# A convolution in Winograd form: the weights from two DMA queues, and two image loads made one

## The chip, the cores and the metric

The kernel runs on one core of one Trainium2 chip. The metric is the device time of one execution, in microseconds (us); the time of a kernel is the median of its runs. The kernel before takes 126.02 us, the median of three runs (125.92 to 126.29).

## The reference

`x` is 16 images of 64 channels of 64 x 64, `weight` is 128 x 64 x 3 x 3, both float32. The output is the ordinary 3 x 3 convolution with one pixel of zero padding, float32, 16 x 128 x 64 x 64:

```python
x_pad = np.pad(x, ((0, 0), (0, 0), (1, 1), (1, 1)), mode='constant')
for b in range(batch):
    for co in range(c_out):
        for ci in range(c_in):
            for kh in range(3):
                for kw in range(3):
                    output[b, co] += weight[co, ci, kh, kw] * x_pad[b, ci, kh:kh+h, kw:kw+w]
```

The input is 16.8 MB, the weights are 0.29 MB and the output is 33.6 MB.

## The kernel before

**Tiling.** Images are taken in eight pairs, p = 0 to 7. A pair fills the 128 partitions: 64 channels of one image and 64 of the next. Along the rows the kernel uses a Winograd form, which makes two output rows from sums, differences and outer differences of input rows, so that fewer matrix products are needed. Each pair is worked in two halves (h = 0 and 1), so there are 16 halves, in the order of the list `halves` (line 196).

**Memory.** One tile, `homes`, has eleven places of 16 KB for each partition. `X_HOME` says which place receives the input of a pair, and `O_HOME` which two places hold its two output images until they are stored. Places are used again: the output of a pair goes where the inputs of pairs already used were. The fifth pair (p = 4) and the sixth (p = 5) are loaded to the places 7 and 8, which lie next to each other.

**Loads.** At the start SyncE issues all the loads one behind the other on its DMA queue: the weights (line 66; output channel on the partition, 2304 bytes each), pair 0 in two parts (rows 0 to 33, and the rest), and pairs 1 to 7 whole, 2 MB each (line 71). That is ten transfers.

**Weights.** As soon as they are in, GpSimd (line 84) and ScalarE (line 85) each cast them to float16, TensorE transposes them (line 101), and ScalarE and VectorE build seven combinations of them in `Wt` (lines 147 to 158). In between VectorE makes the sums of the first half (line 112, from line 152), which the first matrix products need.

**A half.** GpSimd makes sums (line 112), differences (line 119) and outer differences (line 130) of a half, two halves ahead of its use. ScalarE casts some rows (line 140). TensorE does the products (line 178). ScalarE copies partial results from PSUM to the output's place (lines 245, 247, 249, 263), and VectorE combines (lines 260 to 262).

**Stores.** They are written out by hand in `stores` (line 213): nothing goes out before the half (2, 0). Then SyncE issues a store of half an image and one of a whole image; after (2, 1) four more; and from then on a pair at a time (`store_both`, line 207). The last seven rows of one image of pair 5 are stored by two transfers from ScalarE's queue (lines 252 and 253). The ones before are all on SyncE's queue, behind the loads.

**Order.** `keep` fixes the order of the instructions of each engine as written. The framework gives each transfer from SyncE or ScalarE one of eight semaphores in turn, in the order in which they stand in the program; a transfer that takes a semaphore again waits until the one that had it before has landed. So the ninth and tenth transfers wait for the first and the second.

Of the kernel before, what the change touches and what calls it, by code (L numbers as in the profile page):

```python
# [15 lines left out]
def kernel(  # L16
# [12 lines left out]
    nc = tc.nc  # L29
# [3 lines left out]
    NP = B // 2  # L33
    RB = 8

    keep = tc.keep_in_program_order
    x_rows = x.rearrange("b c h w -> (b c) h w")
    w_flat = weight.rearrange("co ci kh kw -> co (ci kh kw)")
# [13 lines left out]
    homes = slots.tile([128, 11, H, W], F32)  # L52
# [9 lines left out]
    def spared(at, n):  # L62
        return spare[:, at : at + n]

    w_raw = spared(0, CI * 9)
    keep(nc.sync.dma_start(w_raw, w_flat))

    def load(p, cuts=((0, H),)):
        for lo, hi in cuts:
            keep(  # L70
                nc.sync.dma_start(
                    xs[p][:, lo:hi, :], x_rows[128 * p : 128 * p + 128, lo:hi, :]
                )
            )

    load(0, ((0, 34), (34, H)))
    for p in range(1, NP):
        load(p)

    ident = spared(1920, 64).bitcast(F16)  # L80
# [214 lines left out]
```

## Time and profile before

| | |
|---|---|
| median of three runs | 126.02 us (125.92 to 126.29) |
| the profiled execution | 126.17 us |
| its span, first to last instruction or transfer | 124.3 us |
| busy: TensorE / VectorE / ScalarE / GpSimd | 95.5 / 63.6 / 81.3 / 90.6 us |
| moved by the DMA engines | 50.77 MB, mean 408 GB/s over the span |
| weights: issue, landing | 0.74 us, 3.5 us later |
| first matrix product of the convolution | 8.55 us |
| first store issued | 40.23 us |
| last matrix products end, last store issued | about 104.5 us, 105.82 us |

Times in the trace count from the start of the span. A busy time is that of one engine; the DMA share is the mean over the core's 16 DMA engines. A wait of an engine is put down to what ended last before it went on.

### The profile page before, as it was taken

How to read it: one execution, taken by the hardware profiler on the slowest of the kernel's cores; microseconds unless marked ns; L12 is line 12 of the kernel's file. 1: busy time of each engine (PE TensorE's matmuls, PEld its weight loads, DVE VectorE, ACT ScalarE, POOL GpSimd, SP SyncE). 2: the span in 40 equal slices, each digit the busy share in tenths (PEclk: the TensorE clock that was granted, in tenths of full speed). 3: DMA queues.
4: the chain of work that ended last, by engine and by line, in shares of the span. 5: the costliest groups of instructions: out<-in, count | busy, mean ns of one | idle time of the engine just before them, and what ended most of it. 6: DMA issues, size and time to landing. Idle time of an engine off the chain costs nothing.

```text
span 124.3 us, 2114 instructions
## 1 busy us (share of the span) xinstructions
PE 95.5 (77%) x873; PEld 49.8 (40%) x873; DVE 63.6 (51%) x56; ACT 81.3 (65%) x86; POOL 90.6 (73%) x52
## 2 busy tenths in 40 slices
PE   0329999999999998969999999999999996000000
PEld 0214555555455553534555555555555552000000
DVE  0099848393928472908294837556483939000000
ACT  4466798879697938659979797888888793000000
POOL 2209999999999999999999999999999700000000
PEclk9999999999999999999999999999999999655555
DMA  4999999999999999999999999999999999999980
GB/s 112 388 443 432 443 427 438 417 422 422 427 427 438 411 464 401 432 438 417 422 424 435 438 427 424 422 438 422 431 418 441 416 436 421 421 422 448 427 369 37
DMA packets 3954, 50.77 MB, mean 408 GB/s; under 512 B 360, under 2 KB 488, under 8 KB 744
## 3 DMA queue, kind: packets, MB, share of 16 engines
q1 hardware_dynamic: 3808, 50.40, 95.9%
q10 hardware_dynamic: 136, 0.23, 0.5%
q8 instruction: 7, 0.11, 0.3%
q14 instruction: 3, 0.02, 0.0%
HBM read 17.07 MB, written 33.55 MB: 407 GB/s over the span
## 4 chain that ended last, share of the span: by engine, by line
PE 68%; DMA 10%; DVE 4%; ACT 2%; POOL 1%; issue 0%; ACTq 0%; SPq 0%; DVEq 0%
PE acc L178 68%; DMA out_dram<-homes 7%; DMA homes<-in_weight_dram 3%; DVE homes L262 2%; DVE ss L112 1%; ACT homes L245 1%; ACT homes L247 1%; POOL homes L84 1%; DVE homes L149 0%; DVE Wt L150 0%; PE wp L101 0%; ACT homes L147 0%; ACTq L245 0%; SPq L200 0%; DVEq L150 0%
## 5 line engine op out<-in xcount | busy, mean ns | idle before, releaser
L178 PEld LDWEIGHTS <-Wt 64*128 64x128 f16 x864 | 48.8, 95 | 49.2 <-issue 5.3
L178 PE MATMUL acc<-xh,Wt 64*128 64x504 f16 (+3 forms) x384 | 45.9, 370 | 0.2
L112 POOL TENSOR_TENSOR ss<-homes 128x1024 f16<-128x1024 f32 x15 | 35.4, 2360 | 4.3 <-DMA homes<-in_x_dram 4.3
L260 DVE TENSOR_TENSOR homes<-acc,homes 128x1024 f32<-128x1024 f32 x16 | 19.6, 1224 | 34.9 <-PE acc L178 16.9
L130 POOL TENSOR_TENSOR ee<-homes 128x960 f16<-128x960 f32 (+1 forms) x15 | 35.3, 2350 | 0.0
L178 PE MATMUL acc<-ee,Wt 64*128 64x504 f16 (+1 forms) x192 | 26.5, 377 | 1.5 <-ACT homes L245 1.5
L178 PE MATMUL acc<-ss,Wt 64*128 64x504 f16 (+1 forms) x192 | 24.9, 392 | 2.3 <-DVE ss L112 2.3
L245 ACT COPY homes<-acc 128x1024 f32<-128x1024 f32 x16 | 16.2, 1012 | 10.1 <-DMA out_dram<-homes 4.6
L263 ACT COPY homes<-acc 128x1024 f32<-128x1024 f32 x16 | 16.3, 1017 | 8.5 <-PE acc L178 8.5
L262 DVE TENSOR_TENSOR homes<-homes,acc 128x1024 f32<-128x1024 f32 x16 | 19.5, 1219 | 1.0 <-PE acc L178 0.2
L119 POOL TENSOR_TENSOR dd<-homes 128x512 f16<-128x512 f32 x15 | 20.0, 1332 | 0.0
L261 DVE TENSOR_TENSOR homes<-acc,homes 128x1024 f32<-128x1024 f32 x16 | 19.4, 1214 | 0.0
L140 ACT CAST xh<-homes 128x1088 f16<-128x1088 f32 x16 | 17.9, 1118 | 0.1
L249 ACT COPY homes<-acc 128x1024 f32<-128x1024 f32 x16 | 16.5, 1030 | 0.0
L247 ACT COPY homes<-acc 128x1024 f32<-128x1024 f32 x16 | 16.3, 1017 | 0.3 <-PE acc L178 0.3
L178 PE MATMUL acc<-dd,Wt 64*128 64x504 f16 (+1 forms) x96 | 13.3, 379 | 0.0
L101 PE MATMUL wp<-homes 128*128 128x128 f16 x9 | 1.1, 312 | 5.1 <-POOL homes L84 5.1
L149 DVE SCALAR_TENSOR_TENSOR homes<-wp,homes 128x384 f32<-128x384 f32 x1 | 0.6, 558 | 6.1 <-ACT homes L147 6.1
L101 PEld LDWEIGHTS <-homes 128*128 128x128 f16 x9 | 0.9, 160 | 5.0 <-POOL homes L84 5.0
L84 POOL CAST homes<-homes 128x576 f16<-128x576 f32 x1 | 0.7, 662 | 3.0 <-DMA homes<-in_weight_dram 3.0
L130 DVE TENSOR_TENSOR ee<-homes 128x1088 f16<-128x1088 f32 x1 | 2.5, 2504 | 0.0
L85 ACT CAST homes<-homes 128x576 f16<-128x576 f32 x1 | 0.7, 671 | 2.3 <-DMA homes<-in_weight_dram 2.3
(17 smaller groups left out, 8.2 us busy)
## 6 DMA issues: line engine op xcount, KB each, us to landing
out_dram<-homes SPq DMA_DIRECT2D x5, 4096.0 KB, 21.2
homes<-in_x_dram SPq DMA_DIRECT2D x7, 2048.0 KB, 30.4
out_dram<-homes SPq DMA_DIRECT2D x4, 2048.0 KB, 16.6
out_dram<-homes SPq DMA_DIRECT2D x2, 1024.0 KB, 6.7
out_dram<-homes SPq DMA_DIRECT2D x1, 1824.0 KB, 20.8
homes<-in_x_dram SPq DMA_DIRECT2D x1, 1088.0 KB, 5.6
homes<-in_x_dram SPq DMA_DIRECT2D x1, 960.0 KB, 7.5
homes<-in_weight_dram SPq DMA_DIRECT2D x1, 288.0 KB, 3.5
```

The costliest lines, as they stand in the source:

```text
L112: keep(eng.tensor_add(t, v[:, j : j + 16, 0, :], v[:, j : j + 16, 1, :]))
L119: keep(eng.tensor_sub(t, v[:, j : j + RB, 1, :], v[:, j : j + RB, 0, :]))
L130: eng.tensor_sub(ees[p][:, lo - 16 : hi - 16, :], xs[p][:, lo - 1 : hi - 1, :], xs[p][:, lo + 1 : hi + 1, :],)
L140: keep(nc.scalar.copy(t, xs[p][:, C_ROW[h] : C_ROW[h] + 17, :]))
L178: nc.tensor.matmul(tiles[:, b2, lo:hi, c_lo:c_hi], Wt[p0 : p0 + 64, wi, kw, :], src[p0 : p0 + 64, first : last + 1 : step, c_lo + kw - 1 : ...
L245: keep(nc.scalar.copy(f1, pf1))
L247: keep(nc.scalar.copy(g1, pg1))
L249: keep(nc.scalar.copy(f0, pf2))
L260: keep(nc.vector.tensor_add(g1, pg2, g1))
L261: keep(nc.vector.tensor_add(f0, pf1, f0))
L262: keep(nc.vector.tensor_sub(f1, f1, pf2))
L263: keep(nc.scalar.copy(g0, pg1))
```

## The change

The weights are no longer one transfer of 128 output channels on SyncE's queue. SyncE loads the channels 0 to 63, and ScalarE's queue the channels 64 to 127. Pairs 4 and 5 are no longer two transfers of 2 MB: one transfer of 4 MB fills the places 7 and 8. The count of transfers up to the first store is ten in both kernels.

```diff
     w_raw = spared(0, CI * 9)
-    keep(nc.sync.dma_start(w_raw, w_flat))
+    for eng, lo in ((nc.sync, 0), (nc.scalar, 64)):
+        keep(eng.dma_start(w_raw[lo : lo + 64, :], w_flat[lo : lo + 64, :]))
...
     load(0, ((0, 34), (34, H)))
-    for p in range(1, NP):
+    for p in (1, 2, 3):
+        load(p)
+
+    two = x[8:12, :, :, :].rearrange("(q b) c h w -> (b c) q h w", b=2)
+    keep(nc.sync.dma_start(homes[:, 7:9, :, :], two))
+    for p in (6, 7):
         load(p)
```

## The prediction

> **What bounds the kernel now.** I read the page's rows of slices first, then the chain that ended last, and then asked for busy times by stage. The rows of slices, 40 equal parts of the span:
>
> ```profile
> PE   0329999999999998969999999999999996000000
> POOL 2209999999999999999999999999999700000000
> DMA  4999999999999999999999999999999999999980
> GB/s 112 388 443 432 443 427 438 417 422 422 427 427 438 411 464 401 432 438 417 422 424 435 438 427 424 422 438 422 431 418 441 416 436 421 421 422 448 427 369 37
> ```
>
> TensorE and GpSimd look full, but they are done by slice 34 (about 104 us), and the DMA engines are full from the second slice to the last but one. The span ends when the bytes have been moved. The queue table says whose bytes:
>
> ```profile
> q1 hardware_dynamic: 3808, 50.40, 95.9%
> q10 hardware_dynamic: 136, 0.23, 0.5%
> ```
>
> q1 is SyncE's queue: 50.40 MB of the 50.77, and 95.9% of sixteen engines' span. The chain of waits seems to contradict this, since its heads are TensorE 68% and DMA 10%:
>
> ```profile
> 31 pieces in order of time: start us, us, what
> ...
> 8.55 36.03 PE acc L178 x324
> 44.59 0.02 issue
> 44.61 1.23 DVE homes L262
> 45.84 0.02 SPq L200
> 45.86 0.04 issue
> 45.90 8.33 DMA out_dram<-homes
> ...
> 104.53 1.22 DVE homes L262
> ```
>
> The chain follows instructions back; it stops at the last vector instruction and says nothing of the 18 us of stores behind it. So I don't take TensorE as the bound, and ask the stages for the DMA share (last two columns):
>
> ```profile
> 1.00:2.00 1.00, 0.00 (x0) 0.00 (x0) 0.00 (x0) 1.00 (x1) 0.29 (x1) 1.00 0.29 25
> 2.00:3.00 1.00, 0.00 (x0) 0.00 (x0) 0.00 (x0) 0.01 (x1) 0.00 (x0) 1.00 0.94 266
> 20.00:30.00 10.00, 10.00 (x98) 5.11 (x94) 6.22 (x6) 8.12 (x10) 10.00 (x5) 1.00 1.00 426
> 40.00:42.00 2.00, 2.00 (x22) 1.03 (x20) 0.07 (x1) 2.00 (x3) 2.00 (x1) 1.00 0.96 410
> 120.00:121.00 1.00, 0.00 (x0) 0.00 (x0) 0.00 (x0) 0.00 (x0) 0.00 (x0) 0.50 0.61 262
> 122.00:123.00 1.00, 0.00 (x0) 0.00 (x0) 0.00 (x0) 0.00 (x0) 0.00 (x0) 0.50 0.04 16
> ```
>
> The engines are busy from 2 us on, also where the queue passes from loads to stores (40 to 42 us: 0.96), and they run dry one by one from 120 to 123 us. The trace also holds each DMA packet, which no view lists. From these records: the first weight packet starts at 1.76 us, 1.02 us after its issue at 0.74; a 16 KB packet takes 611 ns and the next one starts at its end; the engines finish between 120.1 and 123.0 us, the slowest alone after 122.6. Only three things can move the end: bytes, time in which an engine has no packet, and where the slowest engine's hiccups lie.
>
> **The frame of the sum.** The profiled execution took 126.17 us: span 124.3, and 1.87 around it. In the span: 1.76 until the first packet, 121.26 of packets on the slowest engine, 1.3 of completion and closing. The median of the runs, 126.02, is 0.15 lower; I add changes to the profiled time and take 0.15 off.
>
> **Bytes.** The same 0.29 MB of weights in packets of 2304 bytes, and the same 4 MB for pairs 4 and 5 in packets of 16 KB. One completion write more for the weights and one fewer for the pairs, 9 ns each per engine. Change: 0.
>
> **Merging pairs 4 and 5.** SyncE saves one issue (328 to 642 ns for the nine loads). All its issues are over at 7.2 us, with data queued until 44 us, so this is worth 0; were the queue empty, it would be worth those 0.3 to 0.6 us. The two pairs now land together:
>
> ```profile
> DMA to landing us min/median/max: 5.6/26.1/37.6
> ```
>
> That is line 71: the first part of pair 0 is issued at 1.18 and lands at 6.8, the last pair is issued at 6.83 and lands at 44.4. By the same view pair 4 lands at about 29.8 (issued 3.76, 26.1 later) and pair 5 at 34.7 (4.36 and 30.4). Pair 4 becomes visible 4.9 us later. Its first user is GpSimd's sum of half (4, 0), the eighth of line 112 on GpSimd, at 51.47 us: 16.8 us of cover. Without that cover the price would be 4.9 us. Is one transfer of 4 MB slower or faster than two of 2 MB? Nearest row: stores of 4 MB with the same pattern of two pieces per partition land every 9.7 us in the packet records, and stores of 2 MB every 4.86, so 0.0 per 4 MB, with ±0.1 for reading.
>
> The semaphores: pairs 6 and 7 are still the ninth and tenth transfers. Before, pair 7's issue waited 1.4 us for the first part of pair 0; now the two wait for the halves of the weights, at the latest 5.1 us (below). Behind them on SyncE's queue stand only the stores, from 40 us on, which keep landed semaphores. 0.
>
> The Trainium skill (DMA: Bandwidth & Descriptors, Anatomy of one DMA) fits a transfer as 2.0 us fixed plus bytes by rate, measured on the software path, and so would credit the merge with 2.0 us if transfers ran one after the other. By it the sum would be 124.0. The shares of 1.00 from 20 to 30 us, with several transfer boundaries in them, say that the fixed part lies under the neighbours' data here.
>
> **Splitting the weights.** SyncE's own issue: 0.39 us for 128 rows; for 64 rows I take 0.33 (the cheapest load) to 0.42. Pair 0's issue stays at 1.1 to 1.2 us. ScalarE now issues a transfer before its table load, which starts at 0.73, lasts 1.28 and is followed by 2.25 us of waiting for the weights. Its two late issues took 0.55 (124 channels) and 1.01 us (4 channels); the table load then ends at 2.6 to 3.0 us, before the cast at 4.26. Hidden; if the weights landed at 2.6 it would cost up to 0.4 on the path of the first product, nothing at the end.
>
> When do the weights land? Now at 4.24 us: fourteen of the sixteen engines have finished their eight rows by 3.25 us, the other two at 3.65 and 3.88, the rest is receipt. Best case, both halves start together at 1.76 and the stragglers vanish: 3.6. Worst case, ScalarE's issue takes 1.01 and its four rows per engine then alternate with packets of pair 0 (328 ns each, 93 for a row): 0.74+1.01+0.63+4x0.42 = 4.06, plus 0.36 of receipt and again one stall of the seen 0.7: 5.1. I take 4.2, no change.
>
> And what is it worth? The first product needs the weights' chain and VectorE's sum, which needs pair 0 (landed 6.8, sum started 7.28). Earlier weights therefore bring the first product forward by at most 0.47 us, later ones push it back one for one, at most 0.9 us. TensorE then runs without a gap to the first store (issued 40.23). With 1.02 from issue to packet that store could start at 41.25; the first engine comes free at 42.15 by the packet records, the slowest at 44.0. Spare: 0.90 us. A delay of 0.9 uses just that, and an earlier store waits for the loads. The next store that waits for products is issued at 45.90 and has its turn at 49.5: 2.6 us spare. All later ones have more (last store issued 105.82, its turn at 110.3). So the landing of the weights is worth 0 at the end in its whole range.
>
> The rule in the Trainium skill that speaks against this half (same page, Rules for kernel authors) is that two transfers to separate halves of the partitions share the same 16 engines and should be one transfer. The trace agrees as far as the shares of the second 2 to 3 us go (0.94 with one queue: there is no idle engine to use); by the rule the landing stays and the sum stays 0.
>
> **What is left is the ramp.** The eight rows of an engine need 8x0.093 = 0.74 us by their usual packet, but 1.2 to 1.5 us pass from the first packet to 2.94 to 3.25, because first packets take 0.14 to 0.70. This 0.45 to 0.75 us is the only piece of the stream that the change touches, and whatever happens to it moves everything behind it, all 121 us, by the same amount. Two queues could overlap their first packets (down to -0.45), or each have a ramp of its own (up to +0.6). Nothing in the trace shows two queues starting on an empty engine; where ScalarE's queue starts beside SyncE's (87.7 us), its packets take their usual 74 ns from the first on, without a pause. That row is the nearest, so I take 0, and keep both ends.
>
> Sum: 126.17 + 0 + 0 + 0 - 0.15 = 126.0.
>
> **Rivals.**
> A. No change, 126.0 (125.65 to 126.4): chance 0.62. 0.3% (0.38 us) is about what a measurement of this kernel can tell from no change; the three runs spread over 0.37.
> B. Slower: the ramp is paid twice. ScalarE's half starts behind, each engine pauses for a second first packet of up to 0.6 us, and the whole stream moves: 126.6 (126.4 to 127.0). It decides once the pause exceeds 0.38. For it: first packets of up to 0.70, and ScalarE's issues of up to 1.01. Against: pair 0 is already queued on SyncE's side from about 2.2 us, so an engine waiting for the other half has something to do. Chance 0.20.
> C. Faster: the ramps overlap and the two straggling engines (0.4 to 0.6 late) are gone: 125.5 (125.2 to 125.64). For it: the slowest engine sets the end, and its lag may come from there. Against: the stragglers at the start need not be the last ones at the end. Chance 0.16.
> D. Faster: the merge removes an exposed pause between two transfers. A transfer has 1.02 us from issue to its first packet and some 0.36 from its last packet to landing; if pair 5 had waited for both, the merge would save 1.4: 124.6. Against: the share of 1.00, which leaves no pause. Chance 0.02.
>
> **How the numbers follow.** The likeliest is A. To hold 8 in 10 the range takes most of B and C: 125.4 to 126.8. Faster 0.18 (C and D), same 0.62, slower 0.20.
>
> **What would show it.** In the profile after: q10 with 0.147 MB more and q1 with as much less; a 4 MB load; the DMA row again full from slice 2 on; weights landed at 3.6 to 5.1; first product at 8.1 to 9.4; first store issued at 39.8 to 41.1; the DMA share from 40 to 42 us still near 1; last store's data ending near 123. Wrong would be: the share from 2 to 3 us far below 0.94 (B) or clearly above (C), a hole at 42 us (then the spare of 0.90 was mis-sized), or a 4 MB load that takes other than 9.7 us.

## The result, and the profile after

The changed kernel takes 127.03 us (median of 14 runs), the kernel before 126.22 (14 runs beside it): 1.0047 times as long, interval 1.0029 to 1.0066. In a second set it was 1.0067 (1.0043 to 1.0091). The forecast was no change, 126.0, with a range up to 126.8. The changed kernel is slower by some 0.6 to 0.85 us.

Four of the 22 executions of the changed kernel took 128.9 to 129.9 us; the ratios, here and below, leave out such executions, and as the recorded profile is of one of them, the lines below are from the run e1, the same kernel profiled again (126.94 us, span 125.2), unless the text says otherwise. The line numbers after the loads are 6 higher than before (L118 for L112, L184 for L178).

First the rows of slices, then the two queues:

```profile
PE   0229999999999999969999999999999996000000
DMA  4999999999999999999999999999999999999991
...
q1 hardware_dynamic: 3728, 50.25, 95.5%
q10 hardware_dynamic: 216, 0.38, 0.9%
```

0.15 MB have moved from q1 to q10, as the diff says. The DMA engines are full as before; so the same bytes take longer. The timeline of the first 10 us shows what came first:

```profile
0.73 0.54 SPq L67 DMA_DIRECT2D homes<-in_weight_dram  x1
0.73 0.57 ACTq L67 DMA_DIRECT2D homes<-in_weight_dram  x1
...
3.43 1.28 ACT L91 ACT_TABLE_LOAD   x1 [3.43 <-DMA homes<-in_weight_dram]
...
4.72 0.67 ACT L91 CAST homes<-homes 128x576 f16<-128x576 f32 x1
...
5.54 1.15 PE L107 MATMUL wp<-homes 128*128 128x128 f16 x9 [5.54 <-ACT homes L91]
```

Each half of 64 channels is issued in 0.54 to 0.57 us, where all 128 took 0.39. And ScalarE's table load, which stood at 0.73 us before, now waits for weights: its idle time ends at 3.43 with the landing of the first half. The cast depends on two transfers now, and a wait for one of them has come to stand ahead of the table load. GpSimd's cast, which has no table load, starts at 3.93 us, when both halves are there; ScalarE's has to wait for the end of the load, 0.79 us longer: its cast starts at 4.72 (4.26 before), and the first product of the convolution at 9.01 (8.55 before). The chain that ended last has it word for word:

```profile
0.73 2.63 DMA homes<-in_weight_dram
...
3.43 1.28 ACT L91
4.71 0.01 issue
4.72 0.68 ACT homes L91
...
9.01 37.10 PE acc L184 x324
```

TensorE's 324 products up to the half (2, 1) take 37.10 us; before, 36.03. The first products, by the timeline of TensorE, after and then before:

```profile
9.01 2.75 PE L184 MATMUL acc<-ss,Wt 64*128 64x512 f16 x12 [2.32 <-DVE ss L118]
11.52 1.51 PE L184 MATMUL acc<-dd,Wt 64*128 64x512 f16 x6
12.80 2.00 PE L184 MATMUL acc<-xh,Wt 64*128 64x512 f16 x12
```

```profile
11.06 0.92 PE L178 MATMUL acc<-dd,Wt 64*128 64x512 f16 x6
11.81 1.47 PE L178 MATMUL acc<-xh,Wt 64*128 64x512 f16 x12
```

The products begin at about half their later speed in both kernels (a pair starts every 0.43 us, later every 0.22), and the slow stretch lasts longer after: the first pair at the later speed starts at 13.98 us, against 11.38. The granted clock is 1.00 in both, so the profile's clock row doesn't show it. The Trainium skill (TensorE: Matmul & The Clock Gate, Part 1) has a free-running window of activity behind such a start, so that the length of the slow stretch depends on where the first products fall in it; these runs agree in that the stretch differs from run to run, from 2.8 us (before) to 5.9 (e14, the kernel before with another order of stores), and do not show the window itself. The first store is issued at 41.75 us, 1.52 later than before: 0.46 from the first product and 1.06 from TensorE.

How much of this is the change's? Seven of the recorded kernels start like the kernel before: itself, e4, e5, e6, e9, e10 and e14. In the other six the casts of the weights start at 3.57 to 3.84 us and not at 4.26, the first product at 7.91 to 8.24 and not at 8.55, and the slow stretch lasts 3.3 to 5.9 us and not 2.8. e9 is one of them:

```profile
3.60 0.67 ACT L85 CAST homes<-homes 128x576 f16<-128x576 f32 x1 [1.59 <-DMA homes<-in_weight_dram]
...
7.98 2.74 PE L178 MATMUL acc<-ss,Wt 64*128 64x512 f16 x12 [2.41 <-DVE ss L112]
...
11.77 2.39 PE L178 MATMUL acc<-xh,Wt 64*128 64x512 f16 x12
```

So the profile before has the latest weights and the shortest slow stretch of the seven. Against their mean (8.13 us) the first product of the kernels with the halves on two queues and the late table load, e1, e11 and e13, comes 0.9 us later (8.97 to 9.08), and not 0.46. The slow stretch isn't longer in these three (4.2 us on the mean, against 4.3 in the seven), so the 1.06 us are scatter and not the change. VectorE has half (2, 0) ready for the first store at 39.84 to 41.08 us in the seven, and at 40.77 to 41.60 in the three.

At that point the spare of 0.90 us is gone. By the packet records the first engine has ended its loads at 42.44 (42.15 before), and the store's first packet starts at 42.59. So some engines wait, 0.03 us on the mean of the sixteen; in the DMA shares of a microsecond it can't be seen:

```profile
42.00:43.00 1.00, 1.00 (x14) 0.50 (x11) 0.00 (x0) 1.00 (x3) 1.00 (x2) 1.00 0.96 401
```

But from there on packets are longer: those of 16 KB last 621.2 ns on average up to 119 us (614.9 before), 107 for each engine, 0.67 us. The lengthening is spread from 44 to 112 us; from 112 to 119 us they last 613 ns in both kernels.

The sum, by the last packet of the slowest engine (124.00 against 123.02, 0.98 later): loads end 0.27 later on the mean of the engines because the first packet came at 2.05 and not at 1.76; the wait at the passage is 0.03 on the mean; the longer packets make 0.67. Together 1.0. The mean of the engines' ends is 1.16 later, so the account is good to some 0.2 us.

### The profile page after: what moved, and what is told of

It reads as the page before. It is cut to its first block, busy times and chain, and to the rows that moved or that the text cites. A ratio compares the mean times of both kernels' runs of the same rounds, so it can differ in the third digit from the quotient of the medians.

```text
span 128.1 us, 2117 instructions
## 1 busy us (share of the span) xinstructions
PE 98.0 (76%) x873; PEld 50.6 (40%) x873; DVE 64.8 (51%) x56; ACT 81.5 (64%) x86; POOL 90.8 (71%) x52
## 4 chain that ended last, share of the span: by engine, by line
PE 68%; DVE 6%; POOL 5%; ACT 3%; DMA 2%; issue 1%; DVEq 0%; POOLq 0%; ACTq 0%
PE acc L184 67%; DMA homes<-in_weight_dram 2%; DVE dd L125 2%; POOL ee L136 2%; POOL ss L118 2%; ACT L91 1%; POOL dd L125 1%; DVE homes L268 1%; DVE ss L118 1%; ACT homes L251 1%; ACT homes L253 1%; ACT homes L91 1%; DVE homes L155 0%; DVE Wt L156 0%; PE wp L107 0%
## 5 line engine op out<-in xcount | busy, mean ns | idle before, releaser
L184 PEld LDWEIGHTS <-Wt 64*128 64x128 f16 x864 | 49.7, 96 | 51.3 <-issue 8.6
L184 PE MATMUL acc<-xh,Wt 64*128 64x504 f16 (+3 forms) x384 | 47.5, 379 | 0.1
L118 POOL TENSOR_TENSOR ss<-homes 128x1024 f16<-128x1024 f32 x15 | 35.3, 2355 | 4.4 <-DMA homes<-in_x_dram 4.4
L136 POOL TENSOR_TENSOR ee<-homes 128x960 f16<-128x960 f32 (+1 forms) x15 | 36.2, 2415 | 0.0
L184 PE MATMUL acc<-ee,Wt 64*128 64x504 f16 (+1 forms) x192 | 27.2, 385 | 1.1 <-ACT homes L251 1.1
L184 PE MATMUL acc<-ss,Wt 64*128 64x504 f16 (+1 forms) x192 | 24.9, 392 | 2.3 <-DVE ss L118 2.3
L125 POOL TENSOR_TENSOR dd<-homes 128x512 f16<-128x512 f32 x15 | 19.4, 1297 | 0.0
L184 PE MATMUL acc<-dd,Wt 64*128 64x504 f16 (+1 forms) x96 | 13.9, 392 | 0.9 <-DVE Wt L162 0.9
L125 DVE TENSOR_TENSOR dd<-homes 128x512 f16<-128x512 f32 x1 | 2.8, 2756 | 0.0
```

The lines of the kernel that those rows point to most:

```text
L118: keep(eng.tensor_add(t, v[:, j : j + 16, 0, :], v[:, j : j + 16, 1, :]))
L125: keep(eng.tensor_sub(t, v[:, j : j + RB, 1, :], v[:, j : j + RB, 0, :]))
L136: eng.tensor_sub(ees[p][:, lo - 16 : hi - 16, :], xs[p][:, lo - 1 : hi - 1, :], xs[p][:, lo + 1 : hi + 1, :],)
L184: nc.tensor.matmul(tiles[:, b2, lo:hi, c_lo:c_hi], Wt[p0 : p0 + 64, wi, kw, :], src[p0 : p0 + 64, first : last + 1 : step, c_lo + kw - 1 : ...
```

## The experiments

All kernels ran beside the kernel before on the same chip. The medians are of all runs of a kernel. "First packet", "store data" (first packet of the store of (2, 1)) and "packets" (mean of 16 KB packets from a microsecond after that to 119 us) are from the packet records of the profiled execution.

| run | median us | ratio to before (interval) | first packet | store data | packets ns |
|---|---|---|---|---|---|
| before | 126.0 to 126.3 | 1 | 1.76 | 42.15 | 614.9 |
| e4 merge alone | 126.14 | 1.0006 (0.9981 to 1.0032) | 1.75 | 42.08 | 616.5 |
| e8 columns, early table | 126.13 | 1.0013 (0.9998 to 1.0027) | 1.75 | 42.24 | 615.0 |
| e2 early table | 126.53 | 1.0033 (1.0016 to 1.0050) | 2.06 | 42.82 | 620.7 |
| e11 columns | 127.10 | 1.0052 (1.0028 to 1.0076) | 1.75 | 42.37 | 621.5 |
| e1 after, again | 127.05 | 1.0067 (1.0043 to 1.0091) | 2.05 | 42.59 | 621.2 |
| e9 store held, 1st copy | 127.04 | 1.0070 (1.0049 to 1.0091) | 1.74 | 43.23 | 622.7 |
| e10 store held, 3rd copy | 129.08 | 1.0220 (1.0183 to 1.0257) | 1.74 | 45.18 | 623.3 |
| e12 split on SyncE, GpSimd waits | 128.14 | 1.0156 (1.0120 to 1.0191) | 2.08 | 43.04 | 619.2 |
| e3 split on SyncE | 128.48 | 1.0141 (1.0113 to 1.0168) | 2.06 | 44.51 | 622.9 |

**e1, the kernel after again.** No edit.

> The kernel after, unchanged, for a profile of one of its usual executions beside the long one that was recorded. Theory T (table load): ScalarE's table load again sits behind the wait for SyncE's half of the weights, its cast starts at about 5.0 us and the first product at 9.3; but GpSimd's first sum does not get ahead of VectorE's first difference, the difference takes about 0.7 us and not 2.8, the first store is issued at 41 to 42 us, and the DMA share has a small dip at 42 to 44 us, some 0.3 to 0.8 us of idle engine time; time 126.6 to 127.0. Theory R (ramp): the first product is late in the same way, but the first store finds its queue still busy, no dip at 42 us, and the stream is late from its first packets on, by the same 0.5 to 0.6 us from 5 us to the end.

Measured 127.05; the profile is the one read above. The table load is where T has it. The dip that T expected at 42 to 44 us is hardly there, and R's late stream is there too, but with 0.3 us and not 0.5 to 0.6. Neither theory has the longer packets; a theory S came from this run.

**e4, the merge alone.**

```diff
-    for eng, lo in ((nc.sync, 0), (nc.scalar, 64)):
-        keep(eng.dma_start(w_raw[lo : lo + 64, :], w_flat[lo : lo + 64, :]))
+    keep(nc.sync.dma_start(w_raw, w_flat))
```

> The weights by one transfer as before, pairs 4 and 5 by one transfer of 4 MB. Theories T and R alike: the merge does nothing, 126.1 to 126.3, first product at 8.55 us. A third theory, that the 4 MB load itself is slower, wants 126.6 to 126.9 here and a landing of the two pairs later than 34.7 us by 0.4 or more.

```profile
L81 SPq DMA_DIRECT2D homes<-in_x_dram x1: 476/476/476, 3.7 to 3.7; - x1
...
DMA to landing us min/median/max: 31.3/31.3/31.3
```

That is the source view of the 4 MB load: issued at 3.72, landed at 35.0, where pair 5 alone had landed at 34.7. The merge costs nothing, as all had expected; the split makes the loss.

**e2, the table load early.**

```diff
+    tiny = const.tile([128, 2], F32)
+    keep(nc.vector.memset(tiny[:, 0:1], 0.0))
+    keep(nc.scalar.copy(tiny[:, 1:2], tiny[:, 0:1]))
```

> The kernel after, and one element that ScalarE copies right behind its issue of the weights, so that the table load comes before any wait for weights. Nothing else changes. Theory T: table load at about 1.3 to 2.6 us, cast at 4.4, first product at 8.6 to 8.7, first store at 40.3 to 40.5, no dip at 42 us; time back to 126.2 to 126.4. Theory R: the first product comes forward as well, but the time stays at 126.7 to 126.9, since the stream of packets starts as late as in the kernel after.

```profile
1.35 1.28 ACT L71 ACT_TABLE_LOAD   x1 [1.35 <-PEq L289]
...
8.47 1.23 DVE L122 TENSOR_TENSOR ss<-homes 128x1024 f16<-128x1024 f32 x1 [1.38 <-DMA homes<-in_x_dram]
```

126.53: half of the loss is back, and less than T wanted. The profiled execution (127.14) is the longest of its eleven runs and shows another wait: one engine was late with pair 0, VectorE's sum waited 1.38 us for it, and the first product came at 9.75. So this run says that the early load helps, and doesn't settle the rest.

**e8 and e11, halves by columns, with and without the early load.** All 128 channels on each queue, 1152 bytes of each; e8 has the early load of e2 besides.

```diff
-    for eng, lo in ((nc.sync, 0), (nc.scalar, 64)):
-        keep(eng.dma_start(w_raw[lo : lo + 64, :], w_flat[lo : lo + 64, :]))
+    for eng, lo in ((nc.sync, 0), (nc.scalar, 288)):
+        keep(eng.dma_start(w_raw[:, lo : lo + 288], w_flat[:, lo : lo + 288]))
```

> The kernel after with the early table load, and the weights halved by columns: each queue loads all 128 output channels, 1152 bytes of each. Theory P (a transfer of 64 partitions is issued more slowly: 0.55 us and its first packet 1.32 us after the start of the issue, against 0.39 and 1.02 for 128 partitions): first packet again at about 1.76 us, the end of pair 0's first part 0.3 us earlier than with halves of 64 channels, time 126.1 to 126.3. Theory Q (two queues at the start cost the 0.3 us): first packet at 2.05 us as in the kernel after, 126.4 to 126.7.

> The kernel after with the weights halved by columns (128 partitions in each half), without the early table load: what the late table load costs when the stream of packets starts on time. Theory T: table load at 3.3 to 3.7 us, cast at 4.6 to 5.0, first product at 8.6 to 9.3, first store at 41.0 to 41.8, time 126.3 to 126.6, between the 126.13 of the columns with the early load and the 127.0 of the kernel after. If the load's place were without effect: 126.1.

The issues of e8, by its timeline:

```profile
0.73 0.43 ACTq L67 DMA_DIRECT2D homes<-in_weight_dram  x1
0.73 0.38 SPq L67 DMA_DIRECT2D homes<-in_weight_dram  x1
```

Two queues start at once, each is issued in 0.38 to 0.43 us, and the first packet is at 1.75. So it is the 64 partitions, not the second queue, that delay the stream by 0.3 us (P, not Q). With the early load this kernel can't be told from the one before (126.13). e11 is the decisive one: it is e8 without the early load. The table load of e8, and under it that of e11:

```profile
1.19 1.28 ACT L71 ACT_TABLE_LOAD   x1 [1.19 <-PEq L289]
```

```profile
3.39 1.28 ACT L91 ACT_TABLE_LOAD   x1 [3.39 <-DMA homes<-in_weight_dram]
```

In e11 the stream starts on time, only the table load is late, and the loss is whole, 1.0052. Its first product comes at 8.97 (8.08 in e8) and its first store is issued at 41.52 (40.12). T's price (126.3 to 126.6) was too low, as T counted idle time alone: the engines wait 0.02 us on the mean at the passage, and the packets behind it are 6.6 ns longer than before. The losses of e2 (late stream) and e11 (late table load) add up to more than that of the kernel with both; the intervals, some 0.2% either way, don't settle how they combine.

**e3, both halves on SyncE, and e12, with GpSimd held back.**

```diff
-    for eng, lo in ((nc.sync, 0), (nc.scalar, 64)):
+    for eng, lo in ((nc.sync, 0), (nc.sync, 64)):
...
+    after_d0 = const.tile([128, 1], F16)
+    keep(nc.gpsimd.tensor_copy(after_d0, d0[:, 0, 0:1]))
     tr[0, 1] = transforms(nc.gpsimd, 0, 1)
```

(The second part is e12 alone.)

> The kernel after, with both halves of the weights issued by SyncE one behind the other: two transfers and two waits, but one queue. Theory T: the table load still waits for the first half, first product at about 9.0 to 9.3, time 126.6 to 127.0 as the kernel after. Theory R: with one queue there is one ramp, the stream starts as before, time 126.1 to 126.3.

> The kernel with both halves of the weights on SyncE (128.48 us), in which GpSimd's first sum of the second half waits for VectorE's first difference by one small copy. In that kernel's profile the sum began at 10.06, the difference at 10.46 and took 2.50 us and not 0.68, TensorE waited 0.61 us and went on at its slow rate until about 16. Theory L (whoever of the two begins first keeps the other out): difference 0.7 us, VectorE's next instructions 1.8 us earlier, first store 1.5 to 2.5 us before the 43.66 of that kernel, time 126.8 to 127.3. If the long difference were not what costs: 128.3 to 128.8.

e3 missed both expectations, 128.48. Its timeline, and under it that of e12:

```profile
0.73 1.18 SPq L67 DMA_DIRECT2D homes<-in_weight_dram  x2
...
10.06 2.35 POOL L118 TENSOR_TENSOR ss<-homes 128x1024 f16<-128x1024 f32 x1 [4.80 <-DMA homes<-in_x_dram]
...
10.46 2.50 DVE L125 TENSOR_TENSOR dd<-homes 128x512 f16<-128x512 f32 x1
```

```profile
10.08 0.68 DVE L125 TENSOR_TENSOR dd<-homes 128x512 f16<-128x512 f32 x1
10.82 0.19 POOL L167 COPY after_d<-dd 128x1 f16<-128x1 f16 x1 [5.94 <-DVE dd L125]
```

With two slow issues in a row pair 0 is issued at 1.96 and the whole stream is 0.85 late. And VectorE's first difference, begun 0.40 us behind GpSimd's sum, ends 0.55 us behind it. Held apart, it takes 0.68, and the first store comes at 41.95 and not at 43.66. The Trainium skill (SBUF — State Buffer, Who interferes with whom) says that a VectorE instruction with two inputs in SBUF contends with a GpSimd one that reads SBUF, and that whichever is issued first blocks the other; the pair of runs agrees. In time nothing is gained: 128.14 us is between the two expectations, and the ratios are 1.0156 and 1.0141. In e12 no engine waits at the passage (the first store packet starts at 43.04, when the first engine ends its loads), and 0.85 us of late stream don't explain a loss of 1.9. This run is not understood.

**e9 and e10, only the first stores later.** The kernel before, and in half (2, 1), behind ScalarE's first copy (e9) or third (e10):

```diff
+    def first_stores():
+        keep(nc.scalar.copy(mark[:, 0:1], Wt[:, 0, 0, 0:1]))
+        keep(nc.sync.dma_start(mark[:, 1:2], mark[:, 0:1]))
+        store(2, 1, 0, 32)
+        store(0, 0)
```

> The kernel before, but the first two stores wait for a one-column transfer on SyncE's queue that in turn waits for ScalarE's first copy of half (2, 1). No compute engine gets more than one small copy; the first store goes from 40.2 to about 41.4 us, its data can come at about 42.4, the first engine is free at 42.15. Theory H (only idle time at the passage counts): 126.2 to 126.3. Theory S (engines that wait start together and their packets are longer from then on): 126.6 to 126.9, with packets of 16 KB at 620 ns and more on average between 60 and 110 us.

> The same with ScalarE's third copy: the first store at about 43.2 us, data at 44.2, a wait of 2.0 us on the first engine and 1.4 on average. Theory H: 127.4 to 127.6. Theory S: 128.0 to 128.3. If a late first store were harmless, 126.2.

The DMA shares (last two columns) of e9, and then e10, at the passage:

```profile
42.00:43.00 1.00, 1.00 (x14) 0.54 (x11) 0.01 (x1) 1.00 (x2) 1.00 (x2) 1.00 0.27 82
43.00:44.00 1.00, 1.00 (x14) 0.46 (x11) 1.00 (x1) 1.00 (x2) 1.00 (x2) 1.00 0.94 385
```

```profile
43.00:44.00 1.00, 1.00 (x12) 0.54 (x10) 0.88 (x1) 1.00 (x3) 1.00 (x2) 1.00 0.08 33
44.00:45.00 1.00, 1.00 (x14) 0.46 (x10) 1.00 (x2) 0.55 (x2) 1.00 (x1) 1.00 0.08 1
```

The code of the weights, loads and products is that of before, and the first store was issued at 42.2 and at 44.2 us, a microsecond later than meant; by the packet records the engines waited 0.70 and 2.55 us on the mean. Both times lie above what either theory expected. In the profiles the packets last 622.7 and 623.3 ns. In e9 that makes 0.82 us (1692 packets in 16 engines, 7.8 ns more than before), with the wait 1.5; in e10, in the same way, 3.4. By the medians the loss is less, 0.75 us in e9 (interval 0.6 to 1.15) and 2.8 in e10 (2.3 to 3.25): hardly more than the waits alone, as H has it. The profiled executions took 127.46 and 129.57 us and are longer than the medians by 0.4 to 0.5, so how long the packets are in the others isn't known.

In the table the packets fall into two groups, 615 to 617 ns where the store was there in time, 621 to 623 where some engine waited for it; but e12, where none waited, has 619.2. So S isn't shown. In e1 and e11, whose profiled executions are near their medians, the waits are 0.03 and 0.02 us and the longer packets make most of the loss; what makes them longer, the wait or the later products that came with it, stays open. Nor do the engines begin the store in step, as S had it: in e1 their first store packets are spread from 42.59 to 44.18 us, before from 42.15 to 44.05.

**e5 and e6, the first store later by VectorE.** The kernel before, and one (e5) or three (e6) copies `nc.vector.tensor_copy(f1, f1)` behind line 262 in half (2, 0).

> The kernel before, and behind VectorE's last instruction of half (2, 0) one copy in place of 128 x 1024 floats, so that the first store is issued 0.6 to 1.2 us later (40.8 to 41.4 us). Weights, loads and products are those of before; VectorE has some 2 us of idle time in each half. Theory H (only the hole at the passage from loads to stores counts): the data of the store can come at 41.9 to 42.4 us, the first engine is free at 42.15, so at most 0.2 us of idle on some engines; time 126.2 to 126.3. Theory S (engines that wait for the first store start it together, and from then on their packets of 16 KB take 620 to 630 ns on average and not 613 to 619): 126.6 to 126.9 if the data come after 42.15 us, with the lengthening spread over 45 to 110 us.

> As the run with one copy, with three: the first store is issued 1.9 to 3.6 us later than in the kernel before (42.1 to 43.8 us) and the engines, which end their loads at 42.15 to 44.0, wait 0.5 to 2.2 us on average. Theory H: 126.7 to 128.3, the time of before and the mean wait. Theory S: 0.6 us on top of that, 127.3 to 128.9. If TensorE's delay from the late weights were needed for the loss, this kernel would show none and stay at 126.2.

148.71 and 150.20 us: no test of the passage, for the copy itself stalled the kernel (e5's VectorE):

```profile
38.62 1.22 DVE L262 TENSOR_TENSOR homes<-homes,acc 128x1024 f32<-128x1024 f32 x1
39.88 23.63 DVE L265 COPY homes<-homes 128x1024 f32<-128x1024 f32 x1
```

It begins while GpSimd works without a gap and ends 0.55 us after the last instruction (60.72 to 62.96) ahead of GpSimd's first pause. In e6 the first copy does the same. e9 and e10 took the place of these runs.

**e7, TensorE kept busy.** The kernel after, with 28 products of the identity ahead of the transposes and 8 of 512 columns behind them, into an unused part of the transposes' PSUM tile.

> The kernel after, with 28 products of the identity matrix while TensorE waits for the weights and 8 more of 512 columns behind the transposes, into a part of PSUM that nothing reads. In the profile of the kernel after the first products of the convolution take 229 ns each and later ones 122; kept busy, TensorE should begin at the short time. The first store then comes 1.3 to 2.5 us earlier, at 39.3 to 40.5 us, in spite of the late table load. Theories H and S: no hole, and what is left is the late first packet: 126.4 to 126.5. Theory R (the start of the stream alone makes the whole loss): 126.8 to 127.0 as the kernel after.

130.40 us, ratio 1.0354 (1.0320 to 1.0388). The eight products took 3.23 us, 0.40 each, so they ran at the slow speed although TensorE had been busy since 1.35 but for 1.0 us ahead of the transposes; VectorE's first step waited for them until 9.86 and the first product came at 14.03. The run made TensorE later instead of earlier and tells nothing of the passage.

**e13 to e15, the first image's store ahead.** The kernels after (e13), before (e14) and of e3 (e15), with

```diff
-        if (p, h) == (2, 0):
+        if (p, h) == (1, 1):
+            store(0, 0)
+        elif (p, h) == (2, 0):
             store(2, 1, 0, 32)
-            store(0, 0)
```

> The kernel after, with the store of the first image (finished at about 20 us) issued behind half (1, 1), ahead of the first store of pair 2, so that a store is queued when the loads end. Weights, table load and products stay as late as in the kernel after. Theory S (the hole and the longer packets behind it make the loss, beside a stream that starts 0.3 us late): first store issued at 28 to 30 us, no dip at 42 us, packets of 16 KB at 615 to 617 ns on average from 45 to 119 us and not 621, time 126.4 to 126.6. If the late products themselves cost: 126.8 to 127.1 as the kernel after.

> The kernel before with the same order of stores. Theory S: there is no hole to close, 126.0 to 126.2, with a smaller spread. If the order of the stores costs something by itself (half (3, 0) waits longer for the place that pair 2 leaves): 126.4 to 127.

> Both halves of the weights on SyncE (128.48 us), with the same order of stores. What is left is the start: pair 0 is issued at 1.96 and not at 1.18 us, and the ends of the loads lay 0.85 us behind those of before. Theory S: 126.9 to 127.2, although VectorE's first difference is late and long there. If the late products cost: 128 and more.

Measured 127.28 (1.0092, 1.0059 to 1.0124), 127.17 (1.0089, 1.0071 to 1.0106) and 127.90 (1.0144, 1.0104 to 1.0184). All three are above what S expected. The order costs 1.2 us by itself, as e14's expectation had left open; its waits say where:

```profile
ACT homes L246 <- DMA out_dram<-homes: 7.2, 1, 7.2
...
PE acc L178 <- ACT homes L246: 5.4, 1, 5.4
```

Half (3, 0) waits 7.2 us for the place that pair 2 leaves, TensorE 5.4 us, and the last store is issued at 111.9 and not at 105.8. Against its own control the changed kernel loses 0.11 us here and not 0.8, and its packets from the passage on are as short (616.5 against 615.9). e15 lies 0.73 us above e14, about the 0.85 by which its stream starts late. So late products cost little where a store is queued when the loads end. That fits S, but the end of these kernels is now set by the late last store, so they don't prove it.

No version beat the kernel before. The nearest, e8, has the same time.

## Why the prediction was wrong

**Right.** The DMA stream is the bound, and the time comes from its start, its waits and its packets. The bytes changed nothing. The merge is worth 0 (e4), with pair 5's landing 0.3 us later and GpSimd's sum of half (4, 0) without a wait. The rule quoted against the split (the Trainium skill, DMA: Bandwidth & Descriptors, Rules for kernel authors) holds: with halves the weights were there for GpSimd's cast at 3.5 to 4.1 us (e1, e2, e8, e11, e13), with one transfer at 3.6 to 3.9 in six runs and 4.3 in the profile before.

**The step that failed first: "Hidden."** The table load was kept at the start of ScalarE's program, behind the new issue: it was to end at 2.6 to 3.0 us, under the wait for the weights. The cover was the wait itself, and the step counted the moved instructions and not the moved waits. With two transfers the cast has two waits, and one of them came to stand ahead of the table load, which thus ended at 4.71. With the stream starting as before, the late load alone is worth the whole loss: e11 has both, e8 has neither.

**Second: "later ones push it back one for one, at most 0.9 us", and so "worth 0 at the end in its whole range".** Cover and spare were read from one execution, the one with the latest weights and the shortest slow stretch of the seven with this start. The first product came 0.46 us later than in that one, well inside the bound, but 0.9 later than the mean of the seven, which is the whole bound. The first store came 1.52 later; the 1.06 beyond the first product are scatter of the slow stretch, which the sum had no term for. From a store's issue to its first packet it took 0.84 to 0.85 us in e1, e2, e3 and e11 (1.02 in e9), where the sum had 1.02, so the spare in the profile before was rather 1.07. By the times at which half (2, 0) was ready, an estimate for the seven is 0.1 to 1.3 us, and 0.9 more uses it up in some of them. The sign for this step was there: the first store was to be issued at 39.8 to 41.1 us, and came at 41.75.

**Third: no price behind the spare.** The sum has no term for what happens when the spare is used up, and the sign that was to show it, a hole at 42 us, didn't come: in e1 the idle time is 0.03 us on the mean, and the longer packets behind it make 0.67. Why they are longer stays open.

**A mis-sized term: SyncE's issue of 64 rows** was taken as 0.33 to 0.42 us, bounded by loads of 128 rows. It is 0.54, ScalarE's 0.57, and the first packet comes 0.29 later. That is the term of rival B ("the ramp is paid twice", up to 0.6), but not by its mechanism: e3 has it with one queue, and e8 doesn't have it with two. B's time, 126.6, is the nearest to the result by luck, for another reason.

## What to carry to other kernels

When a transfer is cut in two, count what waits for it: each consumer gets a second wait, and whatever the program places between the two waits, here a table load of 1.28 us, falls out of its cover. Read a spare ahead of a saturated queue from several executions and at the end of the chain, where it must hold: here the same program had its first store ready up to 1.2 us earlier or later. If a load has to be cut, cutting along the free dimension kept the stream's start here (1.75 us), and cutting across partitions did not (2.05).

## What the runs showed of the hardware

- As the first transfer of a queue, a load of weights to 64 partitions is issued in 0.54 to 0.58 us, one to 128 partitions in 0.38 to 0.43, on either queue, also with half the bytes in each row. From the start of the issue to the first packet it takes 1.32 us and 1.02 on SyncE's queue (e1, e8), 1.78 and 1.31 on ScalarE's, whose half starts last.
- Packets of 16 KB lasted 615 to 617 ns on average in the profiles in which the first store was queued well before the loads ended (before, e4, e8), and 621 to 623 in those in which some engine waited for it, 0.02 to 2.6 us on the mean (e1, e2, e3, e9, e10, e11); e12, where none waited, has 619.2. Which of the things that go with the wait makes them longer isn't shown.
- A VectorE copy of 128 x 1024 floats within SBUF was kept waiting through a whole row of GpSimd instructions, 23.63 us, until GpSimd paused (e5; e6 shows the same). The Trainium skill (SBUF — State Buffer, Who interferes with whom) has the loser blocked for the winner's instruction; here it was blocked for many of them.
- Products of the identity matrix kept TensorE busy from 1.35 to 4.5 us, and after a pause of 1.0 us the transposes, and did not bring it to its faster speed: eight products of 512 columns from 6.50 on still took 0.40 us each (e7).
